# Half-size products of a feed-forward stage: an order written out for four engines, and one more weight buffer

## The chip, the cores and the metric

The kernel runs on one core of a Trainium2 chip. The metric is the device time of one execution in microseconds, as the median of several runs. Beside it there is one profiled execution, whose trace the rows below come from. TensorE is called PE, VectorE DVE, ScalarE ACT, GpSimd POOL or Pool, and SyncE, which issues the loads of weights, SP. PEld is PE's loading of weights.

## The reference, cut to what matters

One layer of an encoder: a mixer with three branches, a cross-attention and a SwiGLU, each behind an RMSNorm, in float32, for 512 tokens of width 1024. The change is in the SwiGLU.

```python
def swiglu(h, w_gate, w_up, w_down):
    return (jax.nn.silu(h @ w_gate) * (h @ w_up)) @ w_down
```

Here `h` is 512 x 1024, `w_gate` and `w_up` are 1024 x 2816, and `w_down` is 2816 x 1024.

## The kernel before, in words

Every matmul is made of three: both operands are cut into a high part of type fp32r and a rest, and high x high, high x low and low x high are added up in PSUM. A cut is two instructions, a copy on ACT (line 105, writes the high part) and a subtraction on DVE (line 106, writes the rest). Weights come in by SP's loads of 1 MB into one of two raw buffers (`wr`, line 113), and are cut into buffers `wh` and `wl`, five of each (lines 118 and 119).

The gate and up projections run over column blocks of 256. Block 0 is done by plain matmuls. For blocks 1 to 10 a scheme with seven half-size products takes the place of eight: weights and activations are split into quarters (for the weights `l11`, `l12`, `l21`, `l22`, each 512 x 128), sums of quarters are formed, and seven products of 512 x 128 by 512 x 256 give the four quarters of the result. The sums of activations (`t1` to `t4`) and the quarters of them (`r11`, `r21`, `r22`) are ready ahead of the stage. Each of the 20 items (10 blocks, gate and up) is one object of the class `Seven`. Its seven products are `l11*r11`, `s1*t1`, `s2*t2`, `l12*r21`, `s3*t3`, `l22*t4` and `s4*r22`. A product is 12 matmuls with 256 columns. Five products run through two accumulating PSUM tiles, `a` (l11, then s2, s3, l22) and `c` (s1, then s4), and l12 has a tile of its own. Between the products ACT copies the running sum out of `a` (`m1`, `u2`, `u3`, line 259), and DVE adds these to the other sums (lines 269 and 283). A gate item ends in three Silu on ACT (lines 879 to 881), an up item in products with the gate on Pool and DVE (lines 884 to 886).

The weight side of an item: Pool forms `s1` = l21 + l22 (line 235) and l11 - l21 in place (237), DVE forms the two other sums in place (238, 239), ACT and DVE cut the left half of the raw tile before the in-place sums (`x`: l11, l12) and after them (`b`: s2, s4), `s1` (`w2`), and the right half (`y`: s3, l22).

The order of an item's instructions is written as `part1` of this item, `last_part` of the item before it, `part2` of this item. But a planner reorders instructions ahead of the run by its own costs of them, so the order on each engine is not the written one. The four PSUM tiles tagged `acc` hold `a` and `c` of two items; block 0 uses the same four (`first`). Behind the stage `split_a` cuts the result, and the object `bd` of class `Back` runs the down projection, with its own loads through the same raw buffers.

Of the kernel before, what the change touches and what calls it, by code (L numbers as in the profile page):

```python
# [8 lines left out]
F32 = mybir.dt.float32  # L9
F32R = mybir.dt.float32r  # L10
AF = mybir.ActivationFunctionType
ALU = mybir.AluOpType
# [5 lines left out]
def encoder_kernel(  # L18
# [9 lines left out]
    nc = tc.nc  # L28
# [42 lines left out]
    zero = cst.tile([P, P], F32, name="zero")  # L71
    nc.vector.memset(zero, 0.0)
# [3 lines left out]
    WARM = 24  # L76
    chan = cst.tile([P, NC_], F32, name="chan")
# [20 lines left out]
    def nm(s):  # L98
        uid[0] += 1
        return f"{s}{uid[0]}"  # L100
# [124 lines left out]

    class Seven:


        def __init__(self, raw, fp, rights, tile_a):
            l11, l12 = raw[:, 0:4, 0:P], raw[:, 4:8, 0:P]  # L230
            l21, l22 = raw[:, 0:4, P:256], raw[:, 4:8, P:256]
            self.fp, self.r, self.tile_a = fp, rights, tile_a
            x = cut(raw, (slice(None), slice(None), slice(0, P)), KD, P)
            s1 = fp.tile([P, 4, P], F32, name=nm("s1"), tag="s1", bufs=1)
            nc.gpsimd.tensor_tensor(out=s1, in0=l21, in1=l22, op=ALU.add)  # L235

            nc.gpsimd.tensor_tensor(out=l21, in0=l11, in1=l21, op=ALU.subtract)  # L237
            nc.vector.tensor_tensor(out=l11, in0=s1, in1=l11, op=ALU.subtract)  # L238
            nc.vector.tensor_tensor(out=l12, in0=l12, in1=l11, op=ALU.subtract)  # L239
            c = tuple(fp.tile([P, 4, P], F32R, name=nm("w2"), tag=f"w2{s}", bufs=2) for s in "hl")  # L240
            split(s1, c[0], c[1])
            b = cut(raw, (slice(None), slice(None), slice(0, P)), KD, P)
            y = cut(raw, (slice(None), slice(None), slice(P, 256)), KD, P)
            lo, hi = (lambda w: tuple(v[:, 0:4] for v in w)), (lambda w: tuple(v[:, 4:8] for v in w))
            self.l = dict(l11=lo(x), l12=hi(x), s1=c, s2=lo(b), s4=hi(b), s3=lo(y), l22=hi(y))

        def mul(self, dst, l, r, first, last):
            lh, ll = self.l[l]
            rh, rl = self.r[r]
            n = 0  # L250
            for w, v in ((lh, rh), (lh, rl), (ll, rh)):
                for k in range(4):
                    nc.tensor.matmul(dst[:, 0:256], w[:, k, :], v[:, k, :], start=first and n == 0,  # L253
                                     stop=last and n == 11, skip_group_check=True)
                    n += 1

        def keep(self, name):
            m = self.fp.tile([P, 256], F32, name=nm(name), tag=name, bufs=2 if name == "u2" else 1)
            nc.scalar.copy(out=m, in_=self.a[:, 0:256])  # L259
            return m  # L260

        def part1(self):
            self.a, self.c = self.tile_a(), self.tile_a()
            self.mul(self.a, "l11", "r11", True, False)
            self.m1 = self.keep("m1")
            self.mul(self.c, "s1", "t1", True, False)

        def part2(self, c11, c22):
            add = lambda o, p, q: nc.vector.tensor_tensor(out=o, in0=p[:, 0:256], in1=q, op=ALU.add)  # L269
            self.mul(self.a, "s2", "t2", False, False)  # L270
            self.u2 = self.keep("u2")
            b = bank(nm("pfb"))
            self.mul(b, "l12", "r21", True, True)
            add(c11, b, self.m1)
            self.mul(self.a, "s3", "t3", False, False)
            u3 = self.keep("u3")
            add(c22, self.c, u3)

        def part3(self, c12):

            self.mul(self.a, "l22", "t4", False, True)
            self.mul(self.c, "s4", "r22", False, True)
            nc.vector.tensor_tensor(out=c12, in0=self.c[:, 0:256], in1=self.u2, op=ALU.add)
            return self.a[:, 0:256]
# [13 lines left out]
    psx["pools"].append((pst, "tp", 6))  # L298
    chr_ = n1.tile([NC_, P], F32, name="chr", bufs=1)
# [8 lines left out]
    def load_wv(c):  # L308
        raw = wp.tile([P, KD, 256], F32, name=nm("wr"), tag="wr", bufs=2)
# [554 lines left out]
    gate = lambda: fp.tile([P, 2, T], F32, name=nm("g"), tag="g", bufs=2)  # L864
    sg = gate()
# [3 lines left out]

    rights = dict(r11=h3q[0][0], r21=h3q[1][0], r22=h3q[1][1])  # L870
    for i in range(4):
        rights[f"t{i + 1}"] = tuple(v[:, i] for v in h3t)
    held = {}

    def last_part(c, which, sv):
        g, af = held[c], afs[c]
        if which == 0:
            p21 = sv.part3(g[:, 0, HT[1]])
            nc.scalar.activation(out=g[:, 0, :], in_=g[:, 0, :], func=AF.Silu)
            nc.scalar.activation(out=g[:, 1, HT[0]], in_=p21, func=AF.Silu)  # L880
            nc.scalar.activation(out=g[:, 1, HT[1]], in_=g[:, 1, HT[1]], func=AF.Silu)
        else:
            p21 = sv.part3(af[:, 0, HT[1]])
            nc.gpsimd.tensor_tensor(out=af[:, 1, HT[1]], in0=af[:, 1, HT[1]], in1=g[:, 1, HT[1]], op=ALU.mult)
            nc.vector.tensor_tensor(out=af[:, 1, HT[0]], in0=p21, in1=g[:, 1, HT[0]], op=ALU.mult)
            nc.gpsimd.tensor_tensor(out=af[:, 0, :], in0=af[:, 0, :], in1=g[:, 0, :], op=ALU.mult)

    open_ = None
    for c in range(1, FH // 256):
        held[c] = gate()  # L890
        for which, w in enumerate((w_gate_ffn, w_up_ffn)):
            raw = load_raw(w[:, c * 256:(c + 1) * 256].rearrange("(k p) n -> p k n", p=P), KD, 256)
            sv = Seven(raw, fp, rights, acc)
            sv.part1()
            if open_:
                last_part(*open_)
            if which == 0:
                sv.part2(held[c][:, 0, HT[0]], held[c][:, 1, HT[1]])
            else:
                sv.part2(afs[c][:, 0, HT[0]], afs[c][:, 1, HT[1]])  # L900
            open_ = (c, which, sv)
    last_part(*open_)
# [79 lines left out]
```

## Time and profile before

| | us |
|---|---|
| median of three runs | 997.5 |
| the three runs | 997.32, 997.5, 1000.11 |
| the profiled execution, its own time | 1005.81 |
| its span in the trace | 1004.1 |

The profiled execution is one run with the profiler on; its own time is slightly longer than the span that the trace covers. Sums made from rows are made against it. The mean granted clock of PE in it was 0.989.

### The profile page before, as it was taken

Reading aid. Unit: us, or ns where it says so; the run is one execution under the profiler, and the core shown is the slowest. Engines: PE = TensorE matmul, PEld = TensorE weight load, DVE = VectorE, ACT = ScalarE, POOL = GpSimd, SP = SyncE. Lnnn points to the kernel's source line nnn. Section 1 sums busy time; section 2 is a strip of 40 time slices with the busy share of each in tenths; the row PEclk is TensorE's granted clock in tenths of the full one; section 3 lists DMA queues with packets and bytes.
Section 4 is the critical chain, followed back from the end, with each engine's and each line's share of the span. In section 5 each row is a group of like instructions: output and inputs, shape, how many; then the busy total and the mean of one; then the engine's idle time right before and its main releaser. Section 6 shows DMA issues by size and latency. Waiting matters only on the chain. (4 is left out here: it accounts for less than half of the span.)

```text
span 1004.1 us, 13477 instructions
## 1 busy us (share of the span) xinstructions
PE 974.7 (97%) x5546; PEld 855.0 (85%) x5546; DVE 577.1 (57%) x719; ACT 433.4 (43%) x652; POOL 192.4 (19%) x175
## 2 busy tenths in 40 slices
PE   7999999999999999999999999999999999899997
PEld 7988888887888888888988887899999998888885
DVE  6586879444232334346646443786888878652213
ACT  5464755334222233355545334554545454542211
POOL 1121113320001212210000000144545454100000
PEclk8999999999999999999999999999999999999999
DMA  7312222124322322351652121223232322423202
GB/s 252 105 64 84 84 85 78 39 85 151 101 84 84 126 85 89 112 219 43 209 167 85 43 84 43 85 64 105 85 127 85 127 85 86 166 84 126 84 22 84
DMA packets 77341, 100.76 MB, mean 100 GB/s; under 512 B 1904, under 2 KB 57248, under 8 KB 77280
## 3 DMA queue, kind: packets, MB, share of 16 engines
q1 hardware_dynamic: 76032, 95.45, 28.4%
q0 software_dynamic: 1248, 4.46, 1.2%
q8 instruction: 43, 0.70, 0.3%
q14 instruction: 18, 0.15, 0.1%
HBM read 97.80 MB, written 2.10 MB: 99 GB/s over the span
## 5 line engine op out<-in xcount | busy, mean ns | idle before, releaser
L106 DVE TENSOR_TENSOR wl<-wr,wh 128x1024 fp32r<-128x1024 f32 x194 | 258.1, 1342 | 230.2 <-ACT wh L105 145.0
L105 ACT CAST wh<-wr 128x1024 fp32r<-128x1024 f32 x194 | 201.0, 1050 | 290.1 <-PE pb L139 77.9
L167 POOL TENSOR_TENSOR rs<-ve,mhalf 128x1 f32<-128x1 f32 x22 | 16.5, 749 | 369.5 <-DVE ve L165 359.8
L620 POOL TENSOR_TENSOR merged<-merged,sg 128x512 f32<-128x512 f32 x16 | 27.7, 1729 | 182.3 <-DVE sg L619 182.3
L139 PE MATMUL pb<-wh,aTh 128*128 128x512 f32 x176 | 55.2, 395 | 2.6 <-ACT aTh L105 2.6
L139 PE MATMUL pb<-wl,aTh 128*128 128x512 f32 x176 | 55.1, 395 | 0.0
L139 PE MATMUL pb<-wh,aTl 128*128 128x512 f32 x176 | 53.7, 389 | 0.0
L235 POOL TENSOR_TENSOR s<-wr 128x512 f32<-128x512 f32 x20 | 34.5, 1725 | 85.6 <-DMA wr<-in_w_gate_ffn_dram 32.7
L139 PE MATMUL pgt<-hTh,wh 128*128 128x512 f32 x192 | 47.6, 390 | 0.0
L139 PE MATMUL pgt<-hTh,wl 128*128 128x512 f32 x192 | 47.4, 389 | 0.0
L139 PE MATMUL pgt<-hTl,wh 128*128 128x512 f32 x192 | 47.4, 389 | 0.0
L253 PE MATMUL pf<-h3th,wh 128*128 128x256 f32 x240 | 38.6, 284 | 5.2 <-ACT u L259 5.2
L139 PEld LDWEIGHTS pgt<-hTh,wh 128*128 128x128 f32 x192 | 36.0, 188 | 7.6 <-DVE ybl L106 0.2
L139 PEld LDWEIGHTS pgt<-hTl,wh 128*128 128x128 f32 x192 | 36.0, 188 | 7.5
L139 PEld LDWEIGHTS pgt<-hTh,wl 128*128 128x128 f32 x192 | 36.1, 188 | 7.5
L139 PEld LDWEIGHTS pb<-wh,aTh 128*128 128x128 f32 x176 | 33.5, 191 | 9.8 <-ACT aTh L105 2.8
L237 POOL TENSOR_TENSOR wr<-wr 128x512 f32<-128x512 f32 x20 | 40.2, 2010 | 0.9
L139 PEld LDWEIGHTS pb<-wl,aTh 128*128 128x128 f32 x176 | 33.6, 191 | 7.2
L478 POOL TENSOR_SCALAR_AFFINE_SELECT ab<-ab 128x128 f32<-128x128 f32 x32 | 23.6, 770 | 80.2 <-ACT ab L475 80.2
L139 PEld LDWEIGHTS pb<-wh,aTl 128*128 128x128 f32 x176 | 33.0, 188 | 6.8
L253 PE MATMUL pf<-h3th,wl 128*128 128x256 f32 x240 | 38.2, 282 | 0.0
L253 PEld LDWEIGHTS pf<-h3th,wh 128*128 128x128 f32 x240 | 32.4, 191 | 6.6 <-ACT u L259 6.6
(273 smaller groups left out, 2134.9 us busy)
## 6 DMA issues: line engine op xcount, KB each, us to landing
wr<-in_w_in_dram SPq DMA_DIRECT2D x26, 1024.0 KB, 5.0
wr<-in_w_gate_ffn_dram SPq DMA_DIRECT2D x11, 1024.0 KB, 6.1
wr<-in_w_up_ffn_dram SPq DMA_DIRECT2D x11, 1024.0 KB, 5.2
wr<-in_w_down_ffn_dram SPq DMA_DIRECT2D x10, 1024.0 KB, 5.0
wr<-in_w_branch_dram SPq DMA_DIRECT2D x6, 1024.0 KB, 4.9
wr<-in_w_out_dram SPq DMA_DIRECT2D x4, 1024.0 KB, 4.9
wr<-in_w_k_xa_dram SPq DMA_DIRECT2D x4, 1024.0 KB
wr<-in_w_v_xa_dram SPq DMA_DIRECT2D x4, 1024.0 KB, 5.0
```

What stands on the lines that cost most here:

```text
L105: nc.scalar.copy(out=hi, in_=src)
L106: nc.vector.tensor_tensor(out=lo, in0=src, in1=hi, op=ALU.subtract)
L139: nc.tensor.matmul(dst, a(i), b(j), start=first and n == 0, stop=last and n == tot - 1)
L167: nc.gpsimd.tensor_tensor(out=rs, in0=ve, in1=mhalf, op=ALU.pow)
L235: nc.gpsimd.tensor_tensor(out=s1, in0=l21, in1=l22, op=ALU.add)
L237: nc.gpsimd.tensor_tensor(out=l21, in0=l11, in1=l21, op=ALU.subtract)
L253: nc.tensor.matmul(dst[:, 0:256], w[:, k, :], v[:, k, :], start=first and n == 0, stop=last and n == 11, skip_group_check=True)
L478: nc.gpsimd.affine_select(out=dg, in_=dg, compare_op=ALU.is_gt, fill=0.0, base=0, channel_multiplier=1, pattern=[[-1, P]])
L620: nc.gpsimd.tensor_tensor(out=merged[:, d, :], in0=merged[:, d, :], in1=sg, op=ALU.add)
```

## The change

The class `Seven` is rewritten. An item now has separate steps: `load`, `sums` (the two Pool sums), `sums2` (the two DVE sums), `hi` and `lo` (ACT's and DVE's half of a cut), `mul` and `keep`. Each instruction in them is handed to `keep_in_program_order` (`pin`), so that the planner leaves the pinned instructions of an engine in the order in which they are written. `seven_run` writes this order as periods. In period k the item n = k is opened, the item p = k-1 is closed, and the weights of q = k+1 are prepared; the load of item k+2 is issued. `seven_open` prepares the first item, and stands ahead of the gating of block 0. The classes `Gate` and `Up` say what is done with each quarter of the result.

The raw buffers go from two to three, `wh` and `wl` from five to six of each, for the whole kernel. The buffers `w2` and `u2` go from two to one. To make room the tile `zero` moves to another pool, and the scratch for Pool's own loads (`dynamic_dma_scratch_size`) is set to 1024. The number of matmuls, cuts, sums and copies in the stage stays the same.

```diff
-        raw = wp.tile([P, a, b], F32, name=nm("wr"), tag="wr", bufs=2)
+        raw = wp.tile([P, a, b], F32, name=nm("wr"), tag="wr", bufs=3)
...
-        h = wp.tile([P, a, b], F32R, name=nm("wh"), tag="wh", bufs=5)
-        l = wp.tile([P, a, b], F32R, name=nm("wl"), tag="wl", bufs=5)
+        h = wp.tile([P, a, b], F32R, name=nm("wh"), tag="wh", bufs=WB)
+        l = wp.tile([P, a, b], F32R, name=nm("wl"), tag="wl", bufs=WB)
...
+        def sums(self):
+
+            r = self.raw
+            self.s1 = self.fp.tile([P, 4, P], F32, name=nm("s1"), tag="s1", bufs=1)
+            pin(nc.gpsimd.tensor_tensor(out=self.s1, in0=r[:, 0:4, P:256], in1=r[:, 4:8, P:256], op=ALU.add))
+            pin(nc.gpsimd.tensor_tensor(out=r[:, 0:4, P:256], in0=r[:, 0:4, 0:P], in1=r[:, 0:4, P:256], op=ALU.subtract))
...
+        def prepare(self):
+
+            x = self.hi(("l11", "l12"), self.left)
+            self.lo(x)
+            self.sums2()
+            c = self.hi(("s1",), self.s1)
+            self.lo(c)
+            b = self.hi(("s2", "s4"), self.left)
+            self.lo(b)
+
+    def seven_open(items):
+        items[0].load()
+        items[0].sums()
+        items[1].load()
+        items[0].prepare()
+
+    def seven_run(items):
+
+        z = len(items)
+        for k in range(z + 1):
+            n = items[k] if k < z else None
+            p = items[k - 1] if k else None
+            q = items[k + 1] if k + 1 < z else None
+            if k + 2 < z:
+                items[k + 2].load()
+            if n:
+                n.a, n.c = n.tile_a(), n.tile_a()
+                n.mul(n.a, "l11", "r11", True, False)
+            if p:
+                u3 = p.keep("u3")
+                p.c22(p.c[:, 0:256], u3)
+            if q:
+                q.sums()
+            if n:
+                y = n.hi(("s3", "l22"), n.right)
+                n.m1 = n.keep("m1")
+                n.lo(y)
+                n.mul(n.c, "s1", "t1", True, False)
+            if p:
+                p.gate22()
+                p.mul(p.c, "s4", "r22", False, True)
+            if q:
+                x = q.hi(("l11", "l12"), q.left)
+                q.lo(x)
+                c = q.hi(("s1",), q.s1)
+            if p:
+                p.c12(p.c[:, 0:256], p.u2)
+            if n:
+                n.mul(n.a, "s2", "t2", False, False)
+                n.u2 = n.keep("u2")
+            if q:
+                q.sums2()
+                q.lo(c)
+            if p:
+                p.done0()
+                p.mul(p.a, "l22", "t4", False, True)
+            if q:
+                b = q.hi(("s2", "s4"), q.left)
+            if p:
+                p.c21(p.a[:, 0:256])
+            if n:
+                bk = bank(nm("pfb"))
+                n.mul(bk, "l12", "r21", True, True)
+            if q:
+                q.lo(b)
+            if n:
+                n.c11(bk[:, 0:256], n.m1)
+                n.mul(n.a, "s3", "t3", False, False)
...
+    class Gate(Seven):
...
+        def c22(self, p, m):
+            self.add(self.g[:, 1, HT[1]], p, m)
+
+        def gate22(self):
+            self.silu(self.g[:, 1, HT[1]], self.g[:, 1, HT[1]])
...
+        def done0(self):
+            self.silu(self.g[:, 0, :], self.g[:, 0, :])
+
+        def c21(self, p):
+            self.silu(self.g[:, 1, HT[0]], p)
...
+    class Up(Gate):
...
+        def gate22(self):
+            self.mul_g(nc.gpsimd, 1, HT[1], None)
...
+        def done0(self):
+            self.mul_g(nc.gpsimd, 0, ALLT, None)
+
+        def c21(self, p):
+            self.mul_g(nc.vector, 1, HT[0], p)
...
+    seven_open(items)
     sg = gate()
     for j in range(2):
         nc.scalar.activation(out=sg[:, j, :], in_=first[j][0], func=AF.Silu)
...
+    seven_run(items)
     close(fp)
...
-    nc = _bacc.Bacc("TRN2", target_bir_lowering=False, num_devices=1)
+    nc = _bacc.Bacc("TRN2", target_bir_lowering=False, num_devices=1, dynamic_dma_scratch_size=1024)
```

## Rows read from the trace of the kernel before

**Rows 1.** The page's strip: PE's busy tenths in 40 slices.

```profile
PE   7999999999999999999999999999999999899997
```

**Rows 2.** Stretches of 10 us: PE, PEld, DVE, ACT, POOL busy (count), PEclk, DMA, GB/s.

```profile
783.00:793.00 10.00, 10.00 (x87) 10.00 (x86) 9.25 (x12) 5.02 (x9) 4.72 (x3) 1.00 0.32 105
...
823.00:833.00 10.00, 10.00 (x91) 10.00 (x90) 9.17 (x12) 4.91 (x8) 4.75 (x3) 1.00 0.19 62
...
843.00:853.00 10.00, 7.77 (x51) 7.37 (x50) 6.62 (x10) 5.78 (x10) 3.48 (x3) 0.83 0.15 48
...
sum 209.70, PE 199.28 PEld 196.00 DVE 169.57 ACT 104.82 POOL 94.04; mean PE 9.49 PEld 9.33 DVE 8.07 ACT 4.99 POOL 4.48
```

**Rows 3.** Timeline of PE: start, us, line, out<-in, count, idle before and releaser.

```profile
663.32 0.64 PE L253 MATMUL pf<-h3h,wh 128*128 128x256 f32 x4
...
738.53 0.62 PE L253 MATMUL pf<-h3th,wh 128*128 128x256 f32 x4
738.98 0.62 PE L253 MATMUL pf<-h3tl,wh 128*128 128x256 f32 x4
...
758.16 0.64 PE L253 MATMUL pf<-h3th,wl 128*128 128x256 f32 x4
758.63 0.63 PE L253 MATMUL pf<-h3th,wh 128*128 128x256 f32 x4
...
872.29 0.62 PE L253 MATMUL pf<-h3h,wl 128*128 128x256 f32 x4
```

**Rows 4.** The chain of work that ended last, around 768 us: start, us, link.

```profile
768.44 5.28 DMA wr<-in_w_gate_ffn_dram
773.88 2.15 POOL s L235
777.00 3.09 PE pf L253 x24
```

**Rows 5.** Timeline of SP's issues of loads.

```profile
728.42 0.37 SPq L114 DMA_DIRECT2D wr<-in_w_gate_ffn_dram  x1
...
829.84 0.37 SPq L114 DMA_DIRECT2D wr<-in_w_gate_ffn_dram  x1
```

**Rows 6.** Instructions of single lines: ns min/median/max, first and last start.

```profile
L106 DVE TENSOR_TENSOR wl<-wr,wh x63: 1206/1226/2326, 665.6 to 872.2; 128x1024 fp32r<-128x1024 f32 x63
...
L106 DVE TENSOR_TENSOR w<-s,w x19: 677/1442/1790, 669.0 to 848.9; 128x512 fp32r<-128x512 f32 x19
...
L239 DVE TENSOR_TENSOR wr<-wr x20: 674/691/1456, 663.0 to 855.6; 128x512 f32<-128x512 f32 x20
...
L269 DVE TENSOR_TENSOR g<-pf,u x10: 411/418/425, 678.6 to 863.2; 128x256 f32<-128x256 f32 x10
...
L105 ACT CAST wh<-wr x63: 1034/1051/1063, 664.5 to 871.1; 128x1024 fp32r<-128x1024 f32 x63
...
L259 ACT COPY u<-pf x40: 350/366/374, 673.2 to 869.5; 128x256 f32<-128x256 f32 x40
...
L235 POOL TENSOR_TENSOR s<-wr x20: 1290/1674/3426, 654.9 to 846.7; 128x512 f32<-128x512 f32 x20
...
L884 POOL TENSOR_TENSOR af<-af,g x10: 731/738/1597, 686.1 to 870.4; 128x256 f32<-128x256 f32 x10
```

**Rows 7.** Timeline of PE ahead of the stage: the hole before 651.91.

```profile
651.91 4.04 PE L139 MATMUL pf<-h3h,wh 128*128 128x256 f32 x32 [0.45 <-ACT h3h L105]
```

**Rows 8.** Behind the stage: the chain's last links, then stretches of 2.5 us.

```profile
868.46 4.93 DMA wr<-in_w_down_ffn_dram
873.47 1.04 ACT wh L105
875.52 117.53 PE pb L139 x510
...
877.50:880.00 2.50, 2.50 (x7) 1.93 (x7) 2.50 (x3) 2.50 (x3) 0.60 (x1) 0.50 0.39 154
880.00:882.50 2.50, 2.50 (x13) 2.05 (x12) 2.50 (x3) 2.50 (x4) 0.00 (x0) 0.98 0.27 107
```

More of the change, by code (lines that the diff above doesn't have):

```diff
@@ L224, in forms_right @@
                 split(f[:, o + j], dst[0][:, o + j, :, ts], dst[1][:, o + j, :, ts])
+    pin = tc.keep_in_program_order
     class Seven:
[L229 to L245, printed above, removed]
@@ new lines, in __init__, with load @@
+        def __init__(self, src, fp, rights, tile_a):
+            self.src, self.fp, self.r, self.tile_a = src, fp, rights, tile_a
+            self.l = {}
+        def load(self):
+            self.raw = load_raw(self.src.rearrange("(k p) n -> p k n", p=P), KD, 256)
+            self.left, self.right = self.raw[:, :, 0:P], self.raw[:, :, P:256]
+        def sums(self):
[3 more added lines that the diff above has]
+            pin(nc.gpsimd.tensor_tensor(out=r[:, 0:4, P:256], in0=r[:, 0:4, 0:P], in1=r[:, 0:4, P:256], op=ALU.subtract))
@@ L252, in mul @@
                 for k in range(4):
-                    nc.tensor.matmul(dst[:, 0:256], w[:, k, :], v[:, k, :], start=first and n == 0,
-                                     stop=last and n == 11, skip_group_check=True)
+                    pin(nc.tensor.matmul(dst[:, 0:256], w[:, k, :], v[:, k, :], start=first and n == 0,
+                                         stop=last and n == 11, skip_group_check=True))
                     n += 1
         def keep(self, name):
-            m = self.fp.tile([P, 256], F32, name=nm(name), tag=name, bufs=2 if name == "u2" else 1)
@@ L259, in keep @@
-            nc.scalar.copy(out=m, in_=self.a[:, 0:256])
-            return m
[L262 to L284, printed above, removed]
+            m = self.fp.tile([P, 256], F32, name=nm(name), tag=name, bufs=1)
+            pin(nc.scalar.copy(out=m, in_=self.a[:, 0:256]))
+            return m
+        def prepare(self):
[6 more added lines that the diff above has]
+            self.lo(b)
@@ L864, in encoder_kernel, with __init__, add, silu @@
     gate = lambda: fp.tile([P, 2, T], F32, name=nm("g"), tag="g", bufs=2)
+    rights = dict(r11=h3q[0][0], r21=h3q[1][0], r22=h3q[1][1])
+    for i in range(4):
+        rights[f"t{i + 1}"] = tuple(v[:, i] for v in h3t)
+    class Gate(Seven):
+        def __init__(self, c, w):
+            super().__init__(w[:, c * 256:(c + 1) * 256], fp, rights, acc)
+            self.af = afs[c]
+        def add(self, o, p, q):
+            pin(nc.vector.tensor_tensor(out=o, in0=p, in1=q, op=ALU.add))
+        def silu(self, o, i):
+            pin(nc.scalar.activation(out=o, in_=i, func=AF.Silu))
+        def c11(self, p, m):
+            self.g = gate()
+            self.add(self.g[:, 0, HT[0]], p, m)
+        def c22(self, p, m):
+            self.add(self.g[:, 1, HT[1]], p, m)
+        def gate22(self):
+            self.silu(self.g[:, 1, HT[1]], self.g[:, 1, HT[1]])
+        def c12(self, p, m):
+            self.add(self.g[:, 0, HT[1]], p, m)
+        def done0(self):
[3 more added lines that the diff above has]
+    class Up(Gate):
+        def mul_g(self, eng, j, cs, p):
+            o = self.af[:, j, cs]
+            pin(eng.tensor_tensor(out=o, in0=o if p is None else p, in1=self.gate.g[:, j, cs], op=ALU.mult))
+        def c11(self, p, m):
+            self.add(self.af[:, 0, HT[0]], p, m)
+        def c22(self, p, m):
+            self.add(self.af[:, 1, HT[1]], p, m)
+        def gate22(self):
+            self.mul_g(nc.gpsimd, 1, HT[1], None)
+        def c12(self, p, m):
+            self.add(self.af[:, 0, HT[1]], p, m)
+        def done0(self):
+            self.mul_g(nc.gpsimd, 0, ALLT, None)
+        def c21(self, p):
+            self.mul_g(nc.vector, 1, HT[0], p)
+    items = []
+    for c in range(1, FH // 256):
+        g, u = Gate(c, w_gate_ffn), Up(c, w_up_ffn)
+        u.gate = g
+        items += [g, u]
+    seven_open(items)
     sg = gate()
@@ L868, in encoder_kernel @@
         nc.vector.tensor_tensor(out=afs[0][:, j, :], in0=first[2 + j][0], in1=sg[:, j, :], op=ALU.mult)
[L870 to L902, printed above, removed]
+    seven_run(items)
     close(fp)
```

24 lines of the change are left out of this document (21 added, 3 removed).

## The prediction, made before the changed kernel ran

> **What bounds the kernel now.** I read the strip by slices first. PE shows 9 nearly everywhere [rows 1], so by busy time nothing is left. But matmuls overlap, and a slice that is full by busy time can hold more or fewer of them, so I went on to counts, in stretches of 10 us inside the feed-forward stage [rows 2]. PE was busy for all of 783 to 793 and all of 823 to 833, yet the first held 87 matmuls and the second 91; 843 to 853 held 51, with PE busy 7.77 us and a granted clock of 0.83, a mean of its two levels, 1.0 (2.4 GHz) and 0.5 (1.2 GHz). So there are three losses: idle time, a lower clock after idle time, and a pace that differs at full clock.
>
> The timeline of PE gives the sizes [rows 3]. The stage's products run from 663.32 to four matmuls after 872.29, that is 872.74: 209.4 us. At the quicker pace four matmuls start every 0.4525 us on average (rows of 738.53 and later: 0.45, 0.45), 113.1 ns each; at the slower every 0.47 (758.16 to 758.63), 117.5 ns. The stage has 20 items (10 column blocks, gate and up) of 7 products of 12 matmuls, 1680 in all; 12 of them ran earlier, so 1668 lie in this stretch. At the quicker pace these need 188.7 us. Over 20 us of the 209.4 are loss.
>
> What ends the waits? The chain of waits [rows 4] shows a load of raw weights (5.28 us), then Pool's sum `s` on it, then the work up to the product that PE waits for. The load can't start sooner, because it waits for one of two raw buffers. SP's issues of the gate loads at 728.42 and 829.84 are five pairs apart [rows 5]: 101.42/10 = 10.14 us per item, where PE alone needs 84 x 0.1131 = 9.50. So the loop buffer, load, Pool, cut, buffer free sets the stage, and its jitter adds the longer holes.
>
> **The change, part by part.** *Third raw buffer and loads written two periods ahead.* The load for item k+2 waits for `y.lo` of item k-1. By the walk below that cut ends some 3 us into period k-1, so the load lands near 3 + 5.3 + issue = 9 us into it, and the first reader (Pool's sums) comes a whole period later. The link load-to-Pool leaves the path; slack about 9 us. Outside this stage the buffers exist too; the chain of waits after the stage is 117.5 us of PE in one piece [rows 8], which a deeper load can't shorten. For the stages ahead I take 0 as well; a load that comes in another's way would cost at most about one landing, 5.3 us [rows 4], and this bound goes for the smaller scratch of Pool's own loads too.
>
> *Fixed order on PE.* A product is 1.36 us. PE's order in a period is l11, s1, (previous item) s4, s2, (previous) l22, l12, s3. Every copy out of the running sum now has at least two other products behind it before PE touches that bank again: 2.7 us, against a copy of 0.37 [rows 6] and the 0.16 us by which a matmul's end trails the start of the next.
>
> *ACT's order* (0 = start of l11): `u3` 0.2 to 0.55; the cut `y.hi` 1.05 [rows 6], to 1.6; `m1` to 2.0; a gate's Silu to 2.4 (I put the three Silus at 0.4, 0.6 and 0.4, by the copies and cuts of their sizes); `x.hi` to 3.45; `s1.hi` (after product s1 at 2.72+0.16) half a cut, to 4.0; `u2` (after s2, 5.43) 5.6 to 6.0; the long Silu to 6.6; `b.hi` to 7.8; the last Silu to 8.2. ACT is busy 104.82/20 = 5.2 us per item [rows 2], so it has room.
>
> *DVE's order.* An add with a PSUM input is 0.42, the two in-place subtractions about 0.69 each, a cut 1.23 at its median (1.21 to 2.33) and the small one 1.44 (0.68 to 1.79) [rows 6]. Walked through with cuts of 1.43, between median and longest: `c22` 0.6 to 1.0; `y.lo` 1.65 to 3.1; `x.lo` 3.5 to 4.9; `c12` to 5.35; two subtractions to 6.75; `s1.lo` to 8.2; an up item's product to 8.6; `b.lo` to 10.0; `c11` to 10.45. The next `c22` is due at 9.5+0.6 = 10.1, so DVE overruns by 0.35 us, and then makes it up, because `y.lo` need not start before 11.15. The PE product that waits for `c22` is s4, due at 2.72: 1.7 us of slack. DVE's busy time of 169.57/20 = 8.48 us per item [rows 2] fits in 9.5, with 1.0 to spare. It is the tightest part.
>
> *Sum of the stage.* 1680 matmuls take 190.0 us at the quicker pace, 197.4 at the slower. Before, the pace changed only where PE had paused; about a third of the undisturbed groups of four ran at the slower one (105 of 317, [rows 3] show one pair of each). With no pauses the stage may stay in either; I take the mix, 192.4. The opening: 12 matmuls that filled a hole before 651.91 [rows 7] now need one of the four banks still held by the first block, so they move behind; that is in the 1680. The hole grows from 0.45 us to nearly 2, which can bring the clock down; one such stretch cost (1-0.83) x 10 = 1.7 us in 843 to 853 [rows 2], so 0 to 1.7. In the first period item 0's cuts and item 1's share DVE, and one late cut of 1.23 is the size of what PE could wait: 0 to 1.2. I take 1.5 for both together. The close: the last item's s4 comes right behind its s3 and waits for `u3` and `c22`: 0.16+0.37+0.42 and their hand-over, 1.3 us, less if later work fills it. Together 195.2, against 209.4: **14.2 us less**.
>
> *What follows.* The down projection starts at 875.52, 2.8 us after the stage. The chain says why: its third load was issued only at 868.46, as the buffer came free, and ACT's cut waited for it until 873.47 [rows 8]. After the wait PE ran on at the low clock (0.50, which is 1.2 GHz), 7 matmuls in 877.5 to 880 where the next 2.5 us held 13. Wait and clock cost up to 4.8 us. With three buffers, and the last raw weights cut early in the last full period, that load lands some 6 us before the end. A cut of a weight buffer freed only by the last product can still stand first on ACT. I take 3 us, between 0 and 4.8.
>
> Gain 14.2 + 3 = 17.2 us on the profiled 1005.81 (its span 1004.1 lies inside): 988.6. The runs' median is 997.5, 8.3 below the profiled execution; I take the same gain off it: 980.3, and say **981**.
>
> **The rivals.** *DVE and Pool stretch each other until DVE is the bound (slower).* The same cut takes 0.677 or 1.79 us, Pool's add 1.29 to 3.43 [rows 6]. If the two never ran side by side, one period would need DVE's unstretched work with two SBUF inputs, 3x1.206+0.677+2x0.674 = 5.64, its adds on PSUM, 3x0.41 and half of one, 1.44, and Pool's two adds and half of its two products, 2x1.29+(1.29+0.73)/2 = 3.59: 10.67 us if no piece of Pool's work falls into DVE's waits or its PSUM adds. The stage would be 213.4+2.8 = 216.2, 6.8 longer; less the 3 us behind it, 1001. It decides from 10.5 us per period. Against it: before, the two had the same work per item and DVE was busy 8.48, not 10.67; for it: the fixed order packs them closer. The Trainium skill (SBUF — State Buffer, Who interferes with whom) says that a DVE instruction with two SBUF inputs contends with a GpSimd instruction that reads SBUF; by that rule, taken strictly, this rival is the forecast, at 1001. The trace agrees in that the same instruction is stretched, but not with so strict a reading.
>
> *DVE holds PE up part of the time.* An overrun above 1.7 us delays s4, so that the period is near 10.0: 200+2.8, 6.6 less than now, with the 3 behind it 988.
>
> *The wait only moves (no change).* `c22` sits behind the previous period's `b.lo` and `c11`; if each period DVE were 2.7 us behind the walk, PE would lose 1.0 at s4, 10.5 per period, and the time would be 997. The walk's overrun of 0.35 speaks against it.
>
> **How the numbers follow.** PE fed, 0.72 (981); held up in part, 0.12 (988); wait moved, 0.06 (997); stretched, 0.10 (1001). A difference under 0.3% can't be told from no change here (the three runs span 997.32 to 1000.11). Faster 0.84, same 0.06, slower 0.10. Range: the best case takes 190.0 with no opening or close and all of 4.8, 24.2 us less, 973. The worst of the likeliest case is the slower pace with 2.9 at the opening, 1.3 at the close and nothing gained behind: 201.6, 7.8 less, 990. With the second rival inside, 973 to 992 holds about 0.8.
>
> **What would show it.** Right: SP's issues 9.5 to 9.9 us per item; 88 to 91 matmuls in every 10 us of the stage with the granted clock at 1.00; hardly any PE wait between the second and the last item; stage 193 to 199 us; the gap behind it under 2 us. Wrong: PE waits for `c22` (an ACT `u` or a DVE add ahead of s4) in most periods; DVE busy above 9.3 of 10 with cuts of a mean near 1.8; Pool's sums running beside every cut; an opening hole followed by a clock of 0.5; PE idle newly outside 650 to 880.

## The result, and the profile after

| | before | changed |
|---|---|---|
| median | 999.98 us (13 runs, 997.32 to 1001.92) | 993.51 us (13 runs, 987.48 to 994.92) |
| profiled execution, its span | 1005.81, 1004.1 | 987.72, 986.0 |

The ratio is 0.9925, with a 95% interval of 0.9904 to 0.9945. So the kernel is faster by 0.75%, which is clear of the noise, and by 6.5 us where 16.5 was forecast. The time lies above the range of 973 to 992. The 13 executions of the changed kernel fall into two groups with nothing between: four at 987.48 to 988.24, nine at 992.76 to 994.92. The profiled one belongs to the first, so what follows here is that group's picture.

The page's strip of PE in 40 slices is digit for digit that of [rows 1]. It doesn't show the change.

Stretches of 10 us answer to [rows 2] (us, PE, PEld, DVE, ACT, POOL busy with counts, granted clock, DMA share, GB/s):

```profile
672.00:682.00 10.00, 8.74 (x62) 8.74 (x63) 7.70 (x11) 4.27 (x8) 5.22 (x3) 0.83 0.32 105
...
783.00:793.00 10.00, 10.00 (x91) 10.00 (x90) 8.94 (x12) 5.38 (x10) 3.92 (x3) 1.00 0.38 126
823.00:833.00 10.00, 10.00 (x91) 10.00 (x90) 8.13 (x11) 5.78 (x11) 4.71 (x4) 1.00 0.33 107
843.00:853.00 10.00, 10.00 (x91) 10.00 (x90) 6.97 (x10) 7.16 (x11) 0.00 (x0) 1.00 0.54 164
```

Where before had 87, 91 and 51 matmuls in the last three stretches, there are now 91 in each. What is missing up to the close is in the opening, in the first line. PE's waits from 661 to 862 us (waiter, releaser: us in total, times, longest) are three, where before had twelve ahead of the one in front of the down projection:

```profile
PE pf L272 <- DVE g L942: 1.9, 1, 1.9
PE pb L138 <- ACT aTh L104: 1.7, 1, 1.7
PE pf L272 <- DVE af L942: 1.0, 1, 1.0
```

Instead of a loop through DMA and Pool [rows 4], the chain that ended last is now PE alone for almost the whole stage (start, us, link):

```profile
707.80 1.36 PE pfb L272 x12
709.16 8.16 PE pf L272 x72
...
841.08 1.36 PE pfb L272 x12
842.44 6.81 PE pf L272 x60
...
853.97 0.34 DVE af L942
...
854.36 2.57 PE pf L272 x20
...
858.05 0.96 ACT aTh L104
...
859.05 3.02 PE pb L138 x12
```

1.36 + 8.16 = 9.52 us per period, again and again. SP's issues of gate loads agree (they answer to [rows 5]): these two are ten items apart, 95.20/10 = 9.52 us where before had 10.14.

```profile
713.23 0.37 SPq L113 DMA_DIRECT2D wr<-in_w_gate_ffn_dram  x1
...
808.43 0.37 SPq L113 DMA_DIRECT2D wr<-in_w_gate_ffn_dram  x1
```

PE's timeline in the opening (start, us, instruction, count, idle before and its releaser) and around the place of [rows 7]:

```profile
650.68 2.55 PE L138 MATMUL pf<-h3h,wh 128*128 128x256 f32 x20 [0.62 <-ACT h3h L104]
...
673.26 0.74 PE L272 MATMUL pf<-h3h,wh 128*128 128x256 f32 x4 [1.89 <-DVE g L942]
...
674.75 1.06 PE L272 MATMUL pf<-h3th,wh 128*128 128x256 f32 x4
```

The hole at 650.68 grew from 0.45 to 0.62 us, not to 2. The pause is elsewhere: 1.89 us before item 0's `s4`, which waits for its `c22`. After it, 16 matmuls took about twice their time, at a granted clock of 0.5.

The spacing of the stage's matmuls, start to start, sorted into the two paces, the low clock and pauses, gives an account of the stage (us; worked out from all starts between the first of the stage and the first of the down projection, against 113.3 ns per matmul). A pause costs a little more than the idle time that the profile shows, since the first matmul behind it is 0.1 us late too.

| | before | changed, profiled | changed, another execution (e1) |
|---|---|---|---|
| the stage | 209.42 | 195.53 | 202.33 |
| its excess at the slow pace | 2.50 | 0.06 | 6.95 |
| its excess at the low clock | 3.01 | 1.60 | 1.50 |
| its pauses (without the gap behind) | 14.9 | 3.5 | 3.5 |
| gap behind the stage | 2.77 | 1.85 | 1.85 |
| from there to the end | 128.59 | 126.96 | 126.97 |

### The profile page after: what moved, and what is told of

It reads as the page before. It is cut to its first block, busy times and chain, and to the rows that moved or that the text cites. A ratio compares the mean times of both kernels' runs of the same rounds, so it can differ in the third digit from the quotient of the medians.

```text
span 986.0 us, 13484 instructions
## 1 busy us (share of the span) xinstructions
PE 964.4 (98%) x5546; PEld 847.5 (86%) x5546; DVE 567.0 (57%) x719; ACT 433.2 (44%) x652; POOL 182.5 (19%) x175
## 5 line engine op out<-in xcount | busy, mean ns | idle before, releaser
L105 DVE TENSOR_TENSOR wl<-wr,wh 128x1024 fp32r<-128x1024 f32 x134 | 164.8, 1236 | 204.6 <-ACT wh L104 129.8
L264 DVE TENSOR_TENSOR wl<-wr,wh 128x1024 fp32r<-128x1024 f32 x60 | 86.5, 1449 | 21.8 <-ACT wh L259 21.8
L278 ACT COPY u<-pf 128x256 f32<-128x256 f32 x40 | 14.9, 373 | 73.6 <-PE pf L272 71.2
L243 POOL TENSOR_TENSOR wr<-wr 128x512 f32<-128x512 f32 x20 | 42.9, 2143 | 1.6
L242 POOL TENSOR_TENSOR s<-wr 128x512 f32<-128x512 f32 x20 | 26.1, 1304 | 72.2 <-DVE w L264 69.9
```

The costliest lines, as they stand in the source:

```text
L105: nc.vector.tensor_tensor(out=lo, in0=src, in1=hi, op=ALU.subtract)
L242: pin(nc.gpsimd.tensor_tensor(out=self.s1, in0=r[:, 0:4, P:256], in1=r[:, 4:8, P:256], op=ALU.add))
L243: pin(nc.gpsimd.tensor_tensor(out=r[:, 0:4, P:256], in0=r[:, 0:4, 0:P], in1=r[:, 0:4, P:256], op=ALU.subtract))
L264: pin(nc.vector.tensor_tensor(out=l, in0=src, in1=h, op=ALU.subtract))
L278: pin(nc.scalar.copy(out=m, in_=self.a[:, 0:256]))
```

## Experiments

Each ratio is to runs of the kernel before on the same chip, with a 95% interval. "Quick" and "slow" are the two paces of the prediction: 113.3 and 117.8 ns from one matmul of 256 columns to the next, both at a granted clock of 1.00.

### Both kernels once more (e1, e2)

No edit.

> The changed kernel unchanged, to see its executions one by one. Pace theory: PE keeps one of its two paces (113.3 or 117.5 ns per matmul) for as long as it doesn't pause, so an execution runs nearly the whole stage at one of them; 1680 matmuls differ by 7.1 us, and the times fall into two groups some 6 us apart (near 987.6 and 994) with next to nothing between. If the profiled execution is of the slower group, its stretches of 10 us hold 87 matmuls each, with PE busy for all of them and no wait between the second and the last period. Wait theory (DVE and Pool stretch each other in the longer executions): the profile of a long execution shows PE waits of 0.3 us or more per period, and the times are spread, not in two groups.

> The kernel before, unchanged, profiled again. If the first profiled execution (1005.8) was an unlucky one, this one is near 1000 and its stage near 204 us instead of 209.4, with fewer stretches at a granted clock of 0.5. If profiling itself costs the kernel before some 6 us, it is near 1006 again with a stage of 209.

The changed kernel again: ratio 0.9911 [0.9878, 0.9943], six executions at 988.11, 988.58, 989.13, 994.33, 994.62 and 995.55. The two groups come back. The profiled one was that of 995.55, and its trace shows what the upper group is (a stretch of 10 us, then PE's timeline behind the opening's pause, at the full clock again):

```profile
823.00:833.00 10.00, 10.00 (x87) 10.00 (x86) 8.93 (x11) 4.64 (x8) 5.45 (x4) 1.00 0.33 106
```

```profile
679.21 0.64 PE L272 MATMUL pf<-h3tl,wh 128*128 128x256 f32 x4
679.68 0.63 PE L272 MATMUL pf<-h3th,wl 128*128 128x256 f32 x4
```

PE is busy for all of the stretch and waits for nothing, but it holds 87 matmuls, not 91. From 679.21 four start every 0.47 us, and so it stays for 1543 matmuls, up to the pause at the close. The same pauses stand in both traces. The stages differ by 202.33 - 195.53 = 6.8 us, and 6.95 - 0.06 = 6.9 of it is pace.

The kernel before, profiled again, took 1002.52, with a stage of 206.76, a gap of 2.95 and 126.95 behind it. So the execution that the prediction started from had 209.42 + 2.77 + 128.59 - 336.66 = 4.1 us more loss there than another one. It is clock: e2's pauses come to 14.9 us too, but its granted clock is 1.00 through the whole stage and for more than 100 us behind it, where the first execution lost 3.0 us to the low clock inside the stage and some 1.6 behind it. (The slow pace and the gap cost e2 0.5 more.) The same pause shows it, for the same Silu in the same period. Here are the first execution, then e2 (a stretch of 3 us and PE's timeline of each):

```profile
849.00:852.00 3.00, 2.79 (x13) 2.79 (x14) 2.92 (x4) 2.78 (x5) 0.57 (x2) 0.56 0.00 0
...
849.21 1.11 PE L253 MATMUL pf<-h3h,wh 128*128 128x256 f32 x4 [2.20 <-ACT g L880]
```

```profile
849.00:852.00 3.00, 3.00 (x27) 3.00 (x27) 2.83 (x5) 2.81 (x5) 0.57 (x2) 1.00 0.00 0
...
848.81 0.74 PE L253 MATMUL pf<-h3h,wh 128*128 128x256 f32 x4 [2.21 <-ACT g L880]
```

After 2.20 us without work the clock fell to 0.5 in one execution, and after 2.21 it stayed at 1.00 in the other.

### Which part of the change takes the waits away (e3 to e7)

e3 and e5: the kernel before with the buffers alone. e6: the third raw buffer alone. e7: the sixth split buffers alone. e4: the changed kernel with two raw buffers. (The smaller scratch and the moved `zero` go with e3, e5 and e6, to make room; e7 has them too. Beside `wh`, `wl` changes likewise, and the raw buffers' number stands at a second load ahead of the stage; these lines are left out here.)

```diff
 e3, e5, e6
-        raw = wp.tile([P, a, b], F32, name=nm("wr"), tag="wr", bufs=2)
+        raw = wp.tile([P, a, b], F32, name=nm("wr"), tag="wr", bufs=3)
 e3, e5, e7
-        h = wp.tile([P, a, b], F32R, name=nm("wh"), tag="wh", bufs=5)
+        h = wp.tile([P, a, b], F32R, name=nm("wh"), tag="wh", bufs=6)
 e4, against the changed kernel
-        raw = wp.tile([P, a, b], F32, name=nm("wr"), tag="wr", bufs=3)
+        raw = wp.tile([P, a, b], F32, name=nm("wr"), tag="wr", bufs=2)
```

> The kernel before with the buffers of the change alone: three raw and six split buffers, the planner's own order. Load theory (the loop buffer, load, Pool, cut sets the stage): the link from the load to Pool leaves the chain, the period falls from 10.1 to under 9.8 us, and the time is 985 to 992. Order theory (the planner's order makes the waits whatever the buffers): the period stays at 10.0 or more and the time is within 0.3% of the kernel before.

> The changed kernel with two raw buffers instead of three. Order theory, by the walk of a period: the load of item k+2 then waits for the cut y of item k, about 3 us into period k, lands near 9 us into it, and is first read at the start of period k+1, so PE is still fed and the time is that of the changed kernel within 0.3% (two groups again). Load theory: Pool's sums wait for the load, the period grows to 10 us or more, and the time is 8 us or more above the changed kernel.

> The kernel with the buffers alone once more, to see whether it really keeps the quick pace. If pace is drawn anew at each pause with the odds seen so far (about 6 in 10 quick), some executions hold a long slow stretch and lie 4 to 6 us above 988; if this order of PE's products favours the quick pace, all lie within 987 to 989.5 again, and the profile shows less than 1 us of slow-pace excess.

> The kernel before with the third raw buffer alone (five split buffers, the planner's order). Load theory (the loop raw buffer, load, Pool set the stage): nearly the whole gain of the buffers, 987 to 991. Split theory (cuts waiting for a free split buffer made the waits): at most a third of it, 995 to 1000.

> The kernel before with the sixth split buffer alone (two raw buffers). Load theory: the period stays near 10.1 us and the time within 0.4% of the kernel before. Split theory: nearly the whole gain, 987 to 991.

| | executions | ratio | stage | pauses | slow-pace excess |
|---|---|---|---|---|---|
| e3 buffers | 987.58 to 988.82 (6) | 0.9883 [0.986, 0.9905] | 195.09 | 5.9 | 0.1 |
| e5 the same | 987.68 to 989.74, one 992.73 (6) | 0.9899 [0.988, 0.9918] | 195.09 | 6.0 | 0.1 |
| e6 third raw | 991.92 to 994.44 (6) | 0.9934 [0.9919, 0.995] | 200.10 | 4.1 | 7.06 |
| e7 sixth split | 999.64 to 1006.93 (12) | 1.0039 [1.0023, 1.0056] | 207.75 | 15.9 | 1.06 |
| e4 order, two raw | 992.01 to 994.05 (5) | 0.9933 [0.9909, 0.9957] | 200.65 | 3.3 | 7.05 |

(Stage, pauses and excess are those of the profiled execution.) The third raw buffer alone takes the pauses from 14.9 to 4.1, in the planner's order. The written order with two raw buffers takes them to 3.3; it was run only with six split buffers, so whether it needs these isn't shown. Either the third raw buffer or the order breaks the loop, and the two together have no fewer pauses than one of them. In e4 the gate loads came 9.90 us per item apart, which is 84 x 117.8 ns, PE's own need at the slow pace. PE's waits inside the stage are three in e6 and two in e4 (e6 first):

```profile
PE pf L251 <- ACT wh L103: 1.6, 1, 1.6
PE pfb L251 <- ACT wh L103: 1.2, 1, 1.2
PE pf L251 <- ACT u L257: 0.5, 1, 0.5
```

```profile
PE pf L272 <- DVE af L942: 1.7, 1, 1.7
...
PE pf L272 <- DVE g L942: 0.7, 1, 0.7
```

The sixth split buffers gain nothing by themselves: e7 is 0.4% slower than before, still has 15.9 of pauses and, as before, waits for Silu and copies (PE's waits from 661 us on):

```profile
PE pf L251 <- ACT g L880: 3.9, 3, 2.0
PE pf L251 <- ACT u L257: 3.1, 6, 0.9
```

e3 and e6 differ in time by pace, not by waits: e6 has fewer pauses and is 5 us slower. The buffers alone are no worse than the whole change: on the same chip e3's median is 988.18 and the changed kernel's 991.73 (e1). One stretch of each, e3 first:

```profile
823.00:833.00 10.00, 10.00 (x91) 10.00 (x90) 8.29 (x10) 5.66 (x11) 5.17 (x3) 1.00 0.34 107
```

```profile
743.00:753.00 10.00, 10.00 (x87) 10.00 (x86) 9.12 (x11) 5.35 (x10) 5.76 (x5) 1.00 0.34 107
```

### The opening (e8)

In the first period, DVE's cut `b.lo` of item 1 is issued behind item 0's `c22`, not ahead of it.

```diff
-            if q:
+            if q and k:
                 q.lo(b)
+            elif q:
+                late = (q, b)
...
                 p.c22(p.c[:, 0:256], u3)
+            if late:
+                late[0].lo(late[1])
+                late = None
```

> The changed kernel, but the DVE half of item 1's cut b is issued after the add c22 of item 0 instead of before it, in the first period alone. Opening theory: PE's wait of 1.9 us at the second period's third product falls under 0.8 us, the granted clock stays at 1.00 behind it, and the stage at the quick pace is 192 to 193 us instead of 195.5, so that a quick execution is near 985 and a slow one near 991. Rival: DVE is behind as a whole, so the wait only moves to the next product that reads a cut, and the stage stays at 195 to 196 (quick) or 202 (slow). Pace theory: with no fall of the clock, the whole stage runs at the pace that the pause at its opening left.

Ratio 0.9893 [0.9862, 0.9924]. Three executions lie at 984.41 to 986.18, three at 992.0 to 993.38. Their middles, 985.11 and 992.79, are 3.0 and 1.4 us below those of the 19 executions of the changed kernel, 988.11 and 994.2; 1.89 + 1.60 = 3.5 was there to win. Between the two traces at the slow pace, e1 and e8, what the stage loses beside that pace fell from 5.0 to 2.1 us; why the slow group's times fell by less isn't shown. The wait of 1.9 is gone from the waits, and so is the low clock; what stays (PE's waits from 661 us on) is a wait of 0.2 one period later, that of 1.0 at the close, and the one behind the stage:

```profile
PE pb L138 <- ACT aTh L104: 1.7, 1, 1.7
PE pf L272 <- DVE af L948: 1.2, 2, 1.0
```

So the opening's loss was `c22` of the first item behind a cut of the second on DVE. In the profiled execution the pace fell to slow at 693.0, behind a break of the stream of some 0.07 us that no wait in the profile explains, and stayed slow for 1402 matmuls.

### What sets the pace (e9, e10, e11, e15, e16)

All go on from e8 and put instructions whose result is read by nobody ahead of `l12`, into the unused half of its PSUM tile. e9: one transposition of 128 columns in every fourth period. e10: one in each. e11: one ordinary matmul of 128 columns in each. e15: two of those. e16: four transpositions in a row in two periods (with the close of the next section).

```diff
                 bk = bank(nm("pfb"))
+                if k % 4 == 3:        # e10: if k
+                    pin(nc.tensor.transpose(bk[:, 256:384], ident, ident))
...
+                if k:                 # e11; e15: two of them
+                    pin(nc.tensor.matmul(bk[:, 256:384], n.l["l12"][0][:, 0, :], n.r["r21"][0][:, 0, 0:P],
+                                         start=True, stop=True, skip_group_check=True))
...
+                for _ in range(4 if k in (3, 11) else 0):    # e16
+                    pin(nc.tensor.transpose(bk[:, 256:384], ident, ident))
                 n.mul(bk, "l12", "r21", True, True)
```

> The order with the late cut, and in five periods (every fourth, from the fourth on) one transposition of the identity by PE into an unused part of a PSUM bank, which nobody reads, ahead of the product l12. Turn theory: in all traces so far PE came out of a group of transpositions at the quick pace (16 of 16 groups), so one of them brings it back to the quick pace, where it stays; the times then form one group near 985 to 986.5, and the profile shows slow stretches only ahead of a transposition. Lottery theory: a transposition is a break like any other, so slow stretches start behind some of them, and the times spread between 985 and 993. Lock theory (pace is fixed by the opening, breaks don't change it): two groups, near 985 and 993.

> The same with one transposition in every period but the first, 19 in all, also read by nobody. It counts outcomes: under the turn theory 19 of 19 stretches behind a transposition are quick, under the lottery theory 10 to 13 of them. The price is 19 times 0.1 to 0.25 us, so 987 to 990 under the turn theory, with one group of times; 989 to 993 under the lottery theory.

> The same places with an ordinary matmul of 128 columns of the same type instead of the transposition, read by nobody. If any change of width brings the quick pace, it does as the transposition does. If it takes the transposition, or a pause, then this matmul costs its 0.06 to 0.1 us, the pace stays as it was, and the times still form two groups near 986 and 994.

> open_late_cut with two matmuls of 128 columns ahead of l12 in every period but the first, where narrow_all had one (their results are read by nobody). They add 19 x 2 x about 60 ns = 2.3 us. Theory of a phase (one such matmul turns the pace over, as the strict alternation of narrow_all showed): two turn it over twice, so the pace stays what it was, and an execution lies near 986.7 or near 994, with no alternation from period to period. Theory of a new draw at every narrow matmul: a mix of paces in each execution, near 990.

> close_no_turn with four 128-column transpositions in a row (result read by nobody) ahead of l12 in two periods, the fourth and the twelfth; in the fourth the last short break of PE is just over. Ahead of the stage, near 638 us, four transpositions in a row stand in every trace taken so far, and the products behind them ran at the quick pace in each. They add 2 x about 0.5 us. Theory that four in a row set the quick pace: all executions lie near 984 + 1 = 985, and the products behind both sites run at 113.3 ns. Theory of the phase (an even number leaves the pace as it was): the pace behind each site is that ahead of it, and the times lie in two groups, near 985 and near 992. Theory of chance: the pace behind a site is free of the one ahead of it, with times in between.

e9: 985.4 to 992.34, ratio 0.9897 [0.9874, 0.992]; its profiled execution, the one of 985.4, was quick behind all five. e10: 987.52 to 988.84, 0.9886 [0.9867, 0.9905]; behind its 19 transpositions the pace was quick 13 times and slow 6 (six of the first ten, none of the last nine). Its times lie in the range of the turn theory, but the trace contradicts it: a transposition doesn't set the quick pace.

The counts from earlier traces in the expectations of e9 and e16 leave out places that speak against both. Behind the four transpositions near 637 us the next starts lie 117.6 to 118.0 ns apart on average in all 19 traces, the slow pace, for the seven matmuls up to the next group; behind that group, near 638 us, they lie 113.4 to 113.5 ns apart, also in all 19. At these two places the pace is the same in every execution; inside the stage it isn't.

e11: 989.68 to 990.99, 0.9908 [0.9886, 0.993]. Here there is a pattern. PE's timeline over the ends of three periods:

```profile
764.48 0.22 PE L348 MATMUL pfb<-h3h,wh 128*128 128x128 f32 x1
764.54 0.69 PE L272 MATMUL pfb<-h3h,wh 128*128 128x256 f32 x4
765.07 0.63 PE L272 MATMUL pfb<-h3l,wh 128*128 128x256 f32 x4
765.54 0.63 PE L272 MATMUL pfb<-h3h,wl 128*128 128x256 f32 x4
...
774.49 0.22 PE L348 MATMUL pfb<-h3h,wh 128*128 128x128 f32 x1
774.55 0.69 PE L272 MATMUL pfb<-h3h,wh 128*128 128x256 f32 x4
775.07 0.62 PE L272 MATMUL pfb<-h3l,wh 128*128 128x256 f32 x4
775.53 0.62 PE L272 MATMUL pfb<-h3h,wl 128*128 128x256 f32 x4
775.98 0.62 PE L272 MATMUL pf<-h3th,wh 128*128 128x256 f32 x4
...
784.14 0.22 PE L348 MATMUL pfb<-h3h,wh 128*128 128x128 f32 x1
```

Behind the narrow matmul at 764.48 four start every 0.47 us; behind the one at 774.49, every 0.455. From one narrow matmul to the next it is 10.01 us, then 9.65. The pace turned over behind each one from 686 us to the end.

e15: 988.68 to 989.88, 0.9896 [0.9882, 0.991]. Two narrow matmuls in a row kept the quick pace in all 19 places of the profiled execution, and each period became 9.76 us, 0.24 more for the two. 19 x 0.24 = 4.6 on the 984.41 of e8 is 989.0, where the four executions lie. That fits a phase that each narrow matmul shifts by one step of two, though no execution of e15 came in at the slow pace, which two should have kept as well.

e16 doesn't fit it: 985.89, 986.4, 986.86, 989.15 and 989.3, ratio 0.9881 [0.9861, 0.9901]. In the profiled one four transpositions turned slow into quick at the first place and left quick as it was at the second. PE's timeline at the first:

```profile
696.02 0.64 PE L272 MATMUL pf<-h3th,wl 128*128 128x256 f32 x4
696.50 0.60 PE L351 MATMUL pfb<-ident 128*128 128x128 f32 x4
...
697.42 0.62 PE L272 MATMUL pfb<-h3l,wh 128*128 128x256 f32 x4
697.87 0.62 PE L272 MATMUL pfb<-h3h,wl 128*128 128x256 f32 x4
```

So four don't leave the pace as it was. Nor is it likely that they always set the quick one: this execution was slow for the 382 matmuls up to the first place, quick behind it, and took 986.4. An execution that is quick from the first place on has no more slow pace to lose, but two of five lie near 989.2. What is left for four in a row is a draw, and what draws is open.

### The close, and whether the quick executions were chance (e12, e13, e14, e17)

In the last period `l22` is issued ahead of `s4`. e12 and e13 are the same kernel, with e9's transpositions; e14 and e17 the same without any.

```diff
             if p:
+                if k == z:
+                    p.mul(p.a, "l22", "t4", False, True)
                 p.gate22()
                 p.mul(p.c, "s4", "r22", False, True)
...
-                p.mul(p.a, "l22", "t4", False, True)
+                if k < z:
+                    p.mul(p.a, "l22", "t4", False, True)
```

> As with the five transpositions, and in the last period PE runs l22 ahead of s4. At the close PE waits for the copy u3 (0.5 us) instead of for the add c22 (1.0 us), so the stage is some 0.5 us shorter than with the five transpositions alone; the rest as there. If DVE or ACT stands in the way at the close, no difference.

> The kernel of turn_few_close once more (transpositions in five periods, whose result nobody reads, a cut fewer in the opening, l22 ahead of s4 in the last period). Its four executions lay at 985.37 to 986.61. Theory of chance (each pause of PE draws the pace anew, the transpositions only make more draws): some executions hold slow stretches, so the times spread from about 985 to 990. Theory of the transposition (it sets the quick pace): all of them lie at 985 to 987 again.

> The same without any transposition: the late cut of the opening put back behind c22, and l22 ahead of s4 in the last period. The close had 1.25 us of pause, and 0.79 with this order, so the quick time is 984.4 - 0.5 = 984. Theory of chance, one draw per stage: two groups, near 984 and, 1668 x 4.5 ns = 7.5 us later, near 991.5. If the order at the close itself decides the pace: one group.

> close_no_turn once more, beside it on the same chip. All five executions of it lay at 990.2 to 991.2, the slow group. If each execution draws the pace by chance, some now lie near 984; if something in this program sets the slow pace, all lie near 991 again.

e12: 985.37 to 986.61 (4), 0.9864 [0.9845, 0.9883]. e13: 987.15 and 987.2, then 990.28 to 992.14 (4), 0.9899 [0.9882, 0.9917]. The program is the same, so it doesn't fix the pace, and e12's four alike were chance or their chip's; in e13's trace the pace behind the first four transpositions was slow, quick, slow and slow. e14: 990.18 to 991.17 (5), 0.991 [0.9897, 0.9924]. e17: 984.8, 984.93, then 990.71 to 991.58 (4), 0.9893 [0.9864, 0.9922]. PE's waits in e14 are two in the whole stage and behind it, 0.5 at the close where the changed kernel had 1.0:

```profile
PE pb L138 <- ACT aTh L104: 1.6, 1, 1.6
PE pf L272 <- ACT u L278: 0.5, 1, 0.5
```

Yet its stage took 198.57, of which 7.43 is slow pace, from 650.8 us, ahead of the stage, to the close. The same program gives 984.8 and 991.6, and nothing between 984.93 and 990.18.

The draw isn't even, nor the same for all programs. Sorted by their times, 7 of 19 executions of the changed kernel were quick (13 and e1's six), 2 of 11 of e14 and e17, 11 of 12 of e3 and e5, none of 11 of e4 and e6. It isn't the chip alone: e3 and e4 ran on one chip, e5 and e6 on another. What in a program shifts the odds wasn't found. No version is shown to be best: e16 (median 986.86), e12 with e13 (987.2 over ten) and e3 with e5 (988.3 over twelve) overlap. These medians lie below the changed kernel's 993.51, but the intervals of the ratios overlap with its own (0.9904 to 0.9945, and 0.9878 to 0.9943 in e1).

## Why the prediction was wrong, point by point

- **The loop.** Buffer, load, Pool and cut did set the stage. The gate loads came 9.52 us apart, not 10.14, and the waits went (e3, e4, e6, the profile after). The prediction gave each part a task of its own, the buffer for the loads and the order for the copies; the third raw buffer or the order is enough for both.
- **The walks.** DVE and ACT kept up, as walked. Between the first item's `s4` and the last item's no wait of PE is left in the profile. The overrun of DVE did no harm.
- **The stage's sum**, 195.2 against 195.53 in the profiled execution, is right by two errors that cancel. The pace took 1680 x 0.1133 + 0.06 = 190.4, not 192.4. The opening took 1.89 idle, 0.3 more behind it and 1.60 at the low clock, 3.8, not 1.5. The close took 1.3, as forecast. The prediction looked for the opening's loss in the hole at 651.91, with a late cut of up to 1.2 beside it; the wait behind that cut was 1.89, and it brought the clock down (e8).
- **Behind the stage** 3 was forecast: the gap fell by 0.92, and what follows it by 128.59 - 126.96 = 1.63, 2.55 in all. The 1.63 is clock, which stayed at 1.00 there, and the change needn't be its cause: e2 took 126.95 from there on without it, behind a gap of 2.95. So of the 3, the runs show the change to give only what the gap lost, 0.9 to 1.1. Another 1.6 came ahead of the stage, which begins at 661.68, not 663.32: the 12 early matmuls moved behind and the hole grew by 0.17 only, which is 1.2 of it, and the first block's matmuls behind the hole took 11.00 us instead of 11.41, by pace. The profiled pair differs by 13.9 + 2.55 + 1.6 = 18.1 us, where 17.2 was forecast: 988.6 on the profiled execution's scale, 987.72 measured. That these are so near is in part luck: this execution drew the quick pace and kept its clock behind the stage.
- **First step that failed: "I take the same gain off" the median.** That took 988.6 to 980.3. The profiled execution of before was 5.8 us above the median of 13, and it lost 4.1 us more in and behind the stage than another execution of the same kernel, e2 at 1002.52, because its clock fell there and e2's didn't. The gain of 17.2 held these microseconds already, as part of the loss in the stage and behind it; taking 17.2 off the median takes them off once more, from executions that need not have them. (Against e2 the stage is 11.2 us shorter, where 14.2 was forecast.) What the rest of the 5.8 was, no trace shows. The other 2.5 of the 8.3 is that the three runs' median, 997.5, lay below that of 13.
- **Second step that failed: "With no pauses the stage may stay in either; I take the mix".** The first half was right, and the second doesn't follow from it: an execution that stays in one pace has no mix. The mix put 2.4 us of slow pace into the stage; the two traces have 0.06 and 6.95. Nine of 13 executions drew the slow one. The median is therefore one of the slow group, 993.5 - 987.7 = 5.8 above the quick profiled execution.
- **The sum of it:** 980.3 + 8.3 (the median) - 0.9 (the stage and around it were better) + 5.8 (the pace) = 993.5.

**The rivals.** DVE did not become the bound: it was busy 41.34 of 50 us, or 7.9 per period of 9.52, in the row below. Single instructions did stretch: the in-place subtraction of line 249 to 1130 ns on average, while Pool's `s` got quicker, 1295 ns (lines by form, 661 to 858 us).

```profile
750.00:800.00 50.00, 50.00 (x443) 50.00 (x442) 41.34 (x49) 28.03 (x48) 22.86 (x16) 1.00 0.32 106
```

```profile
L249 DVE TENSOR_TENSOR wr<-wr 128x512 f32<-128x512 f32 x20 | 22.6, 1130 | 0.7
...
L242 POOL TENSOR_TENSOR s<-wr 128x512 f32<-128x512 f32 x19 | 24.6, 1295 | 69.9 <-DVE w L264 69.9
```

By the rule of the Trainium skill (SBUF — State Buffer, Who interferes with whom), taken strictly, the period would have been 10.67, if no work of Pool fell beside DVE's adds on PSUM; the trace has 9.52. Pair by pair the trace comes close to the rule. In the rows below `s` runs its 1.29, the cut that starts beside it takes 1.93 instead of 1.23, and Pool's subtraction that starts beside the cut takes 2.17, where 1.27 was its shortest before (DVE's timeline, then Pool's):

```profile
728.01 1.93 DVE L264 TENSOR_TENSOR wl<-wr,wh 128x1024 fp32r<-128x1024 f32 x1 [0.19 <-ACT wh L259]
...
727.57 1.29 POOL L242 TENSOR_TENSOR s<-wr 128x512 f32<-128x512 f32 x1 [1.23 <-DVE w L264]
728.94 2.17 POOL L243 TENSOR_TENSOR wr<-wr 128x512 f32<-128x512 f32 x1
```

Over the stage Pool overlaps DVE's instructions without a PSUM input for 52.8 us, and the two engines' stretch, each instruction against the shortest of its shape, is 45.5. What kept the period short is the condition of that rival: Pool also overlaps DVE's adds on PSUM, for 15.2 us (5.9 before), and these keep their 0.41 to 0.43 us. Without the 1.44 for these adds the rival's own sum is 5.64 + 3.59 = 9.23, under 9.52. So the contention is nearly whole where it occurs, and the new order leaves room for it. DVE holding PE up in part, and the wait that only moves, did not come either: PE waits in the second period and the last alone.

## What to carry to other kernels

Count matmuls per stretch beside busy time: PE can be busy for 10 of 10 us, with no wait and the full clock, and still be 4% slow. A forecast goes from one execution to the median only after it is known what makes that execution differ from the median; a loss that the change removes isn't taken off twice. Where a resource shows two rates and the change removes what switches between them, forecast two times with chances, not their mean, and take away one of two causes of a wait before building both.

## What the runs showed of the hardware that was not expected

In this stage a stream of fp32r matmuls of 256 columns, each with its own weights, ran at 113.3 or 117.8 ns per matmul, both at the granted clock 1.00 (2.4 GHz). The `pk` products, matmuls of 256 columns behind 475 us, ran at a third spacing, 119.9 ns, in all 19 traces, at the same clock. By the Trainium skill (TensorE: Matmul & The Clock Gate, Back-to-back issue gap) an isolated gap would be an estimated 256/2.4 + 2.5 = 109.2 ns; all three spacings of the streams lie above it. In the stage the pace changed only at a break of PE's stream, a pause or narrow matmuls in between, and held for 1402 to 1750 matmuls without one. One matmul of 128 columns turned it over each time (e11), two left the quick pace in place (e15), and one transposition did either. Why there are two paces, and why some programs draw the slow one so often, no run here shows. Nor does the length of a pause alone decide the clock: it fell to 0.5 behind waits of 1.89 us (the changed kernel) and 2.20 us (before), and stayed at 1.00 behind one of 2.21 us (e2).
